# Feed-forward down projections: nine of eleven row pairs by seven block products, six pairs' sums made beside gate and up and kept in DRAM

## The chip, the cores and the metric

The kernel runs on one core of a Trainium2 chip. The metric is the device time of one execution in microseconds (us). It computes in float32: every weight block is split into a high and a low part, so that one float32 product takes three matmuls on TensorE (PE): high by high, high by low, low by high.

## The reference, cut to what matters

Two layers (`L = 2`) of an encoder on x of 256 tokens by 1024. Each layer has a feed-forward half step, a mixing block (two attentions and gates, not touched here), and a second feed-forward half step. So a feed-forward block runs four times.

```python
x = x + 0.5 * swiglu(rms_norm(x, ffn1_norm[l]), ffn1_w_gate[l], ffn1_w_up[l], ffn1_w_down[l])
...
x = x + 0.5 * swiglu(rms_norm(x, ffn2_norm[l]), ffn2_w_gate[l], ffn2_w_up[l], ffn2_w_down[l])

def swiglu(x, w_gate, w_up, w_down):
    return (jax.nn.silu(x @ w_gate) * (x @ w_up)) @ w_down
```

`w_gate` and `w_up` are 1024 x 2816, `w_down` is 2816 x 1024.

## The kernel before, in words

A feed-forward block (`ffn`, L305) has two stages.

**Gate and up.** The 2816 hidden columns are cut into eleven chunks of 256 (`NFC`). For each chunk c the loop at L429 loads four pieces of weights, 512 KB each (`columns`, L143; `load`, L137), and multiplies both halves of the tokens with them (`project`, L270): 2 x 24 matmuls of 128x512. ScalarE (ACT) and VectorE (DVE) make the hidden values `hh` from that (L443, L445). Some time later, by a lag counted in blocks of three matmuls (`H_LAG`, and `LAST_LAG` for the last chunk), `turn` (L310) transposes them on PE and splits them.

**Down.** `down` (L372) goes over the same eleven chunks, each now a pair of 128-row blocks of `w_down`. A pair is a product of 2x2 blocks of the tokens' hidden values by 2x2 blocks of weights. The table `PLAN` says how each pair is done:

- S: eight block products, two rows of weights, 24 matmuls (`out_rows`, L286).
- F and G: seven block products (Strassen's scheme in Winograd's form), 21 matmuls (`sevens`, L359, and the loop at L384). They need sums and differences of blocks on both sides. On the side of the hidden values `turn` makes them: seven slots instead of four, by four additions of 128x128 and a larger split. On the side of the weights four differences of 128x512 make two tiles u and v (`differences`, L341).
- G makes u and v in the down stage from the two rows it loads. F has had them made beside gate and up (`prepare`, L352): at the chunks that are keys of `PREP`, for the pair that is the value, two more rows are loaded, u and v are made and split, and both parts stay in SBUF (`stored`). In the down stage an F pair loads only half of its first row and its second row.

The plan before is `SFGFGFGSGSS`: seven pairs by seven products, of which three are F.

**What sets the order.** PE's order is the program's. On the other engines a scheduler orders the instructions; within an engine they run in that order, and each waits for its inputs and for its buffer. All weight loads, also those of `prepare`, are issued from SyncE's queue (SP) into four slots of 512 KB, `raw` (`RAW = 4`). ScalarE makes the high part (L182) and VectorE the low part (L183) into six slots each, `wh` and `wl` (`RING = 6`). A `raw` slot is free when VectorE has read it the last time; a `wh`/`wl` slot when PE has used it. The first block of each seven (`corner`, L363) has a place of its own in the tiles of the normalized tokens. Sums of the hidden values, u, v and the final combination (`combine`, L403) share two buffers, `sums`.

GpSimd (POOL) makes the identity at the start, the reciprocal roots of the norms (`rsqrt`, L172), small work of the attention, and issues six small DMAs.

Of the kernel before, what the change touches and what calls it, by code (L numbers as in the profile page):

```python
# [41 lines left out]
RAW = 4  # L42
LAG = 3
H_LAG, NORM_LAG, QK_LAG, P_LAG, V_LAG, M_LAG = 7.9, 4.0, 16, 10, 7.5, 5.5
LAST_LAG = 6.1
ORDER = ("Q0 Q1 K0 K1 q1 q0 a4 k0 a5 k1 a3 v0 a1 a5 v1 a3 g0 a1 a5 g1 a4 g2 a0 g3 a0 a4 g4 a1 a5 g5 a4 "
         "g6 a0 g7")
FMAX = 3.0e38
IN_W = 4352
HEAD = 128  # L50
PLAN = "SFGFGFGSGSS"
PREP = {2: 1, 5: 3, 8: 5}
NS = sum(kind != "S" for kind in PLAN)


@with_exitstack
def hybrid_encoder(ctx, tc, x, w_gu1, w_d1, w_in, b_gate, qk_gain, rpb, sink, t5,
# [11 lines left out]

    def pad(pool, name, nbytes):  # L70
        nc.vector.memset(pool.tile([P, nbytes // 4], F32, name=name, tag=name, bufs=1), 0.0)

    pad(small, "pad_s", 256)

    wide = act.tile([P, HEAD + D], F32, name="x0", tag="x0")
    gain = wide[:, :3 * L * KD].rearrange("p (n k) -> p n k", n=3 * L)
# [93 lines left out]
        nc.tensor.matmul(ps, xl, wh, start=False, stop=last)  # L170
# [134 lines left out]
    def ffn(l, n, w_gu, w_d, after):  # L305
        with tc.tile_pool(name="ffn", bufs=1) as fp:
# [1 line left out]
            SLOT = ((1, 2), (0, 3))  # L308

            def turn(c, hh):  # L310
                tp = ps_tp.tile([P, 4, P], F32, name="tp", tag="tp")
                for t in range(T):
                    for i in range(2):
                        nc.tensor.transpose(tp[:, SLOT[t][i], :], hh[t][:, i * P:(i + 1) * P], ident)  # L314
                m = 4 if PLAN[c] == "S" else 7
                hi = fp.tile([P, m, P], F32R, name=f"hi{m}", tag=f"hi{m}", bufs=NS if m == 7 else NFC - NS)
                lo = fp.tile([P, m, P], F32R, name=f"lo{m}", tag=f"lo{m}", bufs=NS if m == 7 else NFC - NS)
                if m == 7:
                    a = fp.tile([P, 8, P], F32, name="a", tag="sums", bufs=2)
                    nc.scalar.activation(a[:, :4, :], tp, AF.Copy)  # L320
                    for to, x, y, op in ((4, 0, 3, ALU.add), (6, 1, 0, ALU.subtract), (5, 4, 1, ALU.subtract),
                                         (7, 2, 5, ALU.subtract)):
                        nc.vector.tensor_tensor(a[:, to, :], a[:, x, :], a[:, y, :], op)
                    split_to(hi, lo, a[:, 1:, :])
                else:
                    with tc.high_priority(150 if c == NFC - 1 else 0):
                        split_to(hi, lo, tp)
                hs[c] = (hi, lo)

            def get(t, k):  # L330
# [9 lines left out]

            def differences(r0, r1, into):  # L341
                sub = lambda to, x, y: nc.vector.tensor_tensor(to, x, y, ALU.subtract)  # L342
                u = fp.tile([P, 2, 512], F32, name="u", tag="sums", bufs=2)
# [3 lines left out]
                v = fp.tile([P, 2, 512], F32, name="v", tag="sums", bufs=2)  # L347
# [24 lines left out]
            def down():  # L372
# [4 lines left out]
                while c < NFC:  # L377
                    if PLAN[c] == "S":
                        end = NFC if "S" * (NFC - c) == PLAN[c:] else c + 1
                        out_rows(get, acc, 2 * c, 2 * end, end == NFC, w_d, l, 0.5, after, *rest)  # L380
                        c = end
                        continue
                    final = c == max(PLAN.rindex("F"), PLAN.rindex("G"))
                    for name, slot, (wh, wl) in sevens(c):  # L384
                        if name in banks:
                            t, d = banks[name]
                            first = acc[t][d] is None
                            if first:
                                acc[t][d] = out_bank(t, d)
                            bank = acc[t][d]  # L390
                        else:
                            first = name not in extra
                            if first:
                                pool, tag = (ps_g, "g") if name in "16" else (ps_tp, "tp")
                                extra[name] = pool.tile([P, 512], F32, name=tag, tag=tag)
                            bank = extra[name]
                        three(bank, *[h[:, slot, :] for h in hs[c]], wh, wl, first, final and name in extra)
                        tick(1)
                    if final:
                        rest.append(combine(extra))  # L400
                    c += 1

            def combine(acc):  # L403
                p1, p16 = [fp.tile([P, 2, 512], F32, name=n, tag="sums", bufs=2) for n in ("p1", "p16")]
# [24 lines left out]
            for c in range(NFC):  # L429
# [5 lines left out]
                else:  # L435
                    pieces = columns(w_gu, l, c * 512, 512)
                if c in PREP:
                    prepare(PREP[c])
                pair = []
                for t in range(T):  # L440
                    ps = both[t] if first else project(t, pieces, 512)
# [2 lines left out]
                    hh = fp.tile([P, FC], F32, name="hh", tag="hh", bufs=2)  # L444
                    nc.vector.scalar_tensor_tensor(hh, ps[:, FC:], rstd[t], sg, op0=ALU.mult, op1=ALU.mult)  # L445
# [378 lines left out]
```

## Time and profile before

| what | us |
|---|---|
| median of 3 runs (lowest, highest) | 1088.5 (1087.56, 1088.72) |
| the profiled execution | 1088.83 |
| its span, first to last instruction | 1087.1 |
| second feed-forward block: ten chunks of gate and up | 113.7 (from 372.2 to 485.9) |
| the same block: down | 53.6 (from 490.3 to 543.9) |

One core is profiled; the granted clock of TensorE is 1.000 over the whole span. Times in rows are microseconds from the span's start unless the row says ns. In the table of windows a row holds, for a stretch of time, its length and then the busy time and the number of instructions of PE, PE's weight loads (PEld), DVE, ACT and POOL, then the granted clock, the mean busy share of the 16 DMA engines, and the rate that they moved. In the rows of groups, what stands after the bar is the busy time in us and the mean ns of one, and after the second bar the engine's idle time before them with what ended it. In the rows of DMA issues stand the count, the size of one and the median us from issue to landing. Matmuls overlap, so their rate is read from start to start and not from their duration.

### The profile page before, as it was taken

To read this page: it belongs to the slowest core of one execution; us is meant where nothing else is said; L and a number is where in the kernel's file an instruction comes from. 1 tells how busy PE (TensorE), PEld (TensorE's weight loads), DVE (VectorE), ACT (ScalarE), POOL (GpSimd) and SP (SyncE) were. 2 spreads that over 40 slices of the span, in tenths; PEclk is the share of its full clock that TensorE was granted. 3 is DMA by queue.
4 is the path that set the end of the run, shared out by engine and by line. 5 is a ranking of instruction groups with operands and counts; after the bars stand their busy time and mean duration, and the time that the engine had idled before them with its cause. 6 is when DMAs were issued, how large, how long until landed. Compare 5 with 4: busy or idle time off the path is not lost.

```text
span 1087.1 us, 14699 instructions
## 1 busy us (share of the span) xinstructions
PE 1075.3 (99%) x5137; PEld 891.5 (82%) x5137; DVE 854.8 (79%) x1298; ACT 659.3 (61%) x1002; POOL 116.4 (11%) x118
## 2 busy tenths in 40 slices
PE   9999999999999999999999999999999999999998
PEld 6888888888888888888878888888888888888887
DVE  6888788889886778778877777888888767878785
ACT  6665654788764556565465656457877645656542
POOL 1400000243510000000000000003534000000000
PEclk9999999999999999999999999999999999999999
DMA  7876665755654676666657766547566555776652
GB/s 243 265 218 211 196 200 174 238 186 151 193 179 136 199 227 207 210 203 203 194 174 222 223 211 204 177 155 241 178 188 187 171 169 162 222 241 196 211 167 94
DMA packets 98828, 212.63 MB, mean 196 GB/s; under 512 B 7569, under 2 KB 13745, under 8 KB 98753
## 3 DMA queue, kind: packets, MB, share of 16 engines
q1 hardware_dynamic: 98560, 211.60, 62.3%
q8 instruction: 40, 0.66, 0.2%
q14 instruction: 36, 0.29, 0.1%
q0 software_dynamic: 192, 0.08, 0.1%
HBM read 210.59 MB, written 1.06 MB: 195 GB/s over the span
## 4 chain that ended last, share of the span: by engine, by line
PE 85%; DVE 8%; ACT 3%; issue 3%; DMA 1%; POOL 0%; ACTq 0%; DVEq 0%
PE g L168 19%; PE g L170 19%; PE g L169 18%; PE acc L168 6%; PE acc L170 6%; PE acc L169 6%; DVE wl L183 3%; PE tp L314 2%; ACT wh L182 1%; PE tp L169 1%; PE tp L170 1%; PE tp L168 1%; DMA raw<-in_w_d 1%; PE pt L568 1%; PE sc L547 1%
## 5 line engine op out<-in xcount | busy, mean ns | idle before, releaser
L183 DVE TENSOR_TENSOR wl<-raw,wh 128x1024 fp32r<-128x1024 f32 (+1 forms) x340 | 408.0, 1215 | 75.6 <-ACT wh L182 74.5
L182 ACT ACTIVATE wh<-raw 128x1024 fp32r<-128x1024 f32 (+1 forms) x340 | 348.8, 1044 | 117.4 <-PE g L170 39.3
L168 PE MATMUL g<-wh,xh 128*128 128x512 f32 (+1 forms) x976 | 386.1, 396 | 0.0
L170 PE MATMUL g<-wh,xl 128*128 128x512 f32 (+1 forms) x976 | 378.2, 387 | 0.7 <-DVE xl L183 0.7
L169 PE MATMUL g<-wl,xh 128*128 128x512 f32 (+1 forms) x976 | 377.9, 387 | 0.8 <-DVE wl L183 0.8
L170 PEld LDWEIGHTS g<-wh,xl 128*128 128x128 f32 x976 | 183.4, 188 | 40.8 <-DVE xl L183 2.1
L169 PEld LDWEIGHTS g<-wl,xh 128*128 128x128 f32 x976 | 183.9, 188 | 33.8 <-DVE wl L183 1.6
L168 PEld LDWEIGHTS g<-wh,xh 128*128 128x128 f32 x976 | 183.6, 188 | 32.5 <-DVE hh L445 0.2
L443 ACT ACTIVATE sg<-g,rs_y 128x256 f32<-128x256 f32 x88 | 41.2, 468 | 102.9 <-PE g L170 102.6
L342 DVE TENSOR_TENSOR u<-raw 128x512 f32<-128x512 f32 x56 | 38.5, 690 | 64.5 <-DMA raw<-in_w_d 64.1
L168 PE MATMUL acc<-wh,hi 128*128 128x512 f32 x200 | 78.9, 394 | 0.0
L170 PE MATMUL acc<-wh,lo 128*128 128x512 f32 x200 | 77.9, 390 | 0.0
L169 PE MATMUL acc<-wl,hi 128*128 128x512 f32 x200 | 77.9, 390 | 0.0
L174 POOL TENSOR_TENSOR rs_y<-ms,mhalf 128x1 f32<-128x1 f32 x12 | 6.6, 554 | 657.3 <-DVE ms L220 648.9
L445 DVE SCALAR_TENSOR_TENSOR hh<-g,rs_y,sg 128x256 f32<-128x256 f32 x88 | 42.2, 479 | 28.8 <-ACT sg L443 28.8
L182 ACT ACTIVATE corner<-raw 128x512 fp32r<-128x512 f32 x28 | 17.6, 629 | 62.3 <-DMA raw<-in_w_d 47.0
L560 POOL TENSOR_TENSOR S<-S,sm 128x512 f32<-128x512 f32 x32 | 37.1, 1159 | 71.5 <-DVE sm L559 45.4
L170 PEld LDWEIGHTS acc<-wh,lo 128*128 128x128 f32 x200 | 37.6, 188 | 8.0
L168 PEld LDWEIGHTS acc<-wh,hi 128*128 128x128 f32 x200 | 37.6, 188 | 7.5
L169 PEld LDWEIGHTS acc<-wl,hi 128*128 128x128 f32 x200 | 37.6, 188 | 7.5
L553 ACT ACTIVATE S<-S,mx 128x256 f32<-128x256 f32 x64 | 31.8, 498 | 7.5 <-DVE mx L550 7.4
L174 POOL TENSOR_TENSOR rs_y<-hv,mhalf 128x8 f32<-128x8 f32 (+1 forms) x16 | 27.0, 1693 | 31.4 <-DVE hv L476 28.4
(190 smaller groups left out, 1462.9 us busy)
## 6 DMA issues: line engine op xcount, KB each, us to landing
raw<-in_w_gu SPq DMA_DIRECT2D x176, 512.0 KB, 4.4
raw<-in_w_d SPq DMA_DIRECT2D x100, 512.0 KB, 4.4
raw<-in_w_in SPq DMA_DIRECT2D x64, 512.0 KB, 4.5
raw<-in_w_out SPq DMA_DIRECT2D x16, 512.0 KB, 3.5
bb<-in_b_gate SPq DMA_DIRECT2D x16, 256.0 KB, 3.4
raw<-in_w_bsw SPq DMA_DIRECT2D x8, 512.0 KB, 3.7
raw<-in_w_bna SPq DMA_DIRECT2D x8, 512.0 KB, 3.6
raw<-in_w_d SPq DMA_DIRECT2D x12, 256.0 KB, 2.6
```

Of the source, the lines that this page charges most:

```text
L168: nc.tensor.matmul(ps, xh, wh, start=first, stop=False)
L169: nc.tensor.matmul(ps, xh, wl, start=False, stop=False)
L170: nc.tensor.matmul(ps, xl, wh, start=False, stop=last)
L174: rstd_done[0] = nc.gpsimd.tensor_tensor(y, v, mhalf[:, :n], ALU.pow)
L182: linked("act", lambda: nc.scalar.activation(hi, src, AF.Copy))
L183: linked("dve", lambda: nc.vector.tensor_tensor(lo, src, hi.bitcast(F32), ALU.subtract))
L314: nc.tensor.transpose(tp[:, SLOT[t][i], :], hh[t][:, i * P:(i + 1) * P], ident)
L342: sub = lambda to, x, y: nc.vector.tensor_tensor(to, x, y, ALU.subtract)
L443: nc.scalar.activation(sg, ps[:, :FC], AF.Silu, scale=rstd[t])
L445: nc.vector.scalar_tensor_tensor(hh, ps[:, FC:], rstd[t], sg, op0=ALU.mult, op1=ALU.mult)
L553: nc.scalar.activation(S_[:, t, :], S_[:, t, :], AF.Exp, bias=mx[:, t:t + 1], scale=-1.0, accum_out=sm[:, t:t + 1])
L560: nc.gpsimd.tensor_tensor(S_, S_, sm.unsqueeze(2).to_broadcast([P, T, S]), ALU.mult)
```

## The change

The plan becomes `FHHGHHHHFSS`: nine pairs by seven products, in three kinds. There are two F pairs (0 and 8), one G pair (3) and six of a new kind, H (1, 2, 4, 5, 6, 7); the last two stay S.

- For H, u and v are made beside gate and up as for F, but not split: they are stored to DRAM as they are. In the down stage they are loaded again into `raw` slots and split there. An H pair therefore loads, in the down stage, half a row, a row, u and v: four `raw` slots, where F takes two (half a row and a row), G and S two rows.
- Pairs are prepared at eight chunks (2 to 9) instead of three. Their two rows no longer go through `raw` and SyncE's queue, but through two buffers of their own, `beside`, loaded by DMAs from GpSimd's queue, which also issues the stores of u and v. Per block that is 16 loads and 12 stores of 512 KB on GpSimd's queue.
- The rows of a pair are asked for at the start of a chunk's code and the differences made at its end, behind both `hh`.
- `sums` has three buffers instead of two. To make room, a pad and part of a small tile go, and the scratch for descriptors of GpSimd's DMAs is halved.
- As the plan now begins with a seven-product pair, its accumulators take the banks that the last turn used. The last `turn` transposes into an accumulator bank that is taken ahead (`spare`), with the same lag as the others.

```diff
-PLAN = "SFGFGFGSGSS"
-PREP = {2: 1, 5: 3, 8: 5}
+PLAN = "FHHGHHHHFSS"
+PREP = {2: 0, 3: 1, 4: 2, 5: 8, 6: 4, 7: 5, 8: 6, 9: 7}
+SUMS = 3
...
-    pad(small, "pad_s", 256)
...
-        y = small.tile([P, 24], F32, name="rs_y", tag="rs_y")[:, :n]
+        y = small.tile([P, 8], F32, name="rs_y", tag="rs_y")[:, :n]
...
+    spare = []
+
     def out_bank(t, d):
+        if t and d and spare:
+            return spare.pop()
         tag, n = ACC[t][d]
...
             def turn(c, hh):
-                tp = ps_tp.tile([P, 4, P], F32, name="tp", tag="tp")
+                if c == NFC - 1:
+                    spare.append(out_bank(1, 1))
+                    tp = spare[0].rearrange("p (i n) -> p i n", i=4)
+                else:
+                    tp = ps_tp.tile([P, 4, P], F32, name="tp", tag="tp")
...
-            def prepare(c):
+            def beside(k):
+                r = fp.tile([P, 2, 512], F32, name="beside", tag="beside", bufs=2)
+                nc.gpsimd.dma_start(r, w_d[l, k * P:(k + 1) * P, :].rearrange("p (h n) -> p h n", h=2))
+                return r
+
+            def prepare(c, rows2):
                 def into(name, r):
+                    if PLAN[c] == "H":
+                        kept = dram.tile([P, 2, 512], F32, name=f"{name}{l}{n}{c}")
+                        nc.gpsimd.dma_start(kept, r)
+                        return kept
                     hl = [fp.tile([P, 2, 512], F32R, name=f"{name}{p}{c}", tag=f"{name}{p}{c}") for p in "hl"]
                     split_to(*hl, r)
                     return hl
-                stored[c] = differences(block_row(2 * c), block_row(2 * c + 1), into)
+                stored[c] = differences(*rows2, into)
 
             def sevens(c):
+                def fetched(kept):
+                    r = ring.tile([P, 2, 512], F32, name="raw", tag="raw", bufs=RAW)
+                    nc.sync.dma_start(r, kept)
+                    return parts(r)
...
                 us, vs = stored.get(c) or differences(r0, r1, lambda name, r: parts(r))
+                if PLAN[c] == "H":
+                    us, vs = fetched(us), fetched(vs)
...
                 if c in PREP:
-                    prepare(PREP[c])
+                    rows2 = [beside(2 * PREP[c] + i) for i in range(2)]
...
-                defer(LAST_LAG if c == NFC - 1 else H_LAG, ("h", c), lambda c=c, pair=pair: turn(c, pair))
+                defer(H_LAG, ("h", c), lambda c=c, pair=pair: turn(c, pair))
+                if c in PREP:
+                    prepare(PREP[c], rows2)
...
-    nc = _bacc.Bacc("TRN2", target_bir_lowering=False, num_devices=1, dynamic_dma_scratch_size=2048)
+    nc = _bacc.Bacc("TRN2", target_bir_lowering=False, num_devices=1, dynamic_dma_scratch_size=1024)
```

How the change moves instructions is shown at two places. The first is SyncE's queue in the down stage of the first block, before, from the third pair on (a G pair's two rows, an F pair's half row and row, a G pair's two rows, and so on; L338 is `block_row`, and `raw` is numbered by the program):

```order
L338 DMA raw_1389<-in_w_d1 128x1024
L338 DMA raw_1391<-in_w_d1 128x1024
L338 DMA raw_1435<-in_w_d1 128x512
L338 DMA raw_1437<-in_w_d1 128x1024
L338 DMA raw_1467<-in_w_d1 128x1024
L338 DMA raw_1469<-in_w_d1 128x1024
L338 DMA raw_1513<-in_w_d1 128x512
L338 DMA raw_1515<-in_w_d1 128x1024
```

The same queue now, from the G pair (3) through the first two of the four H pairs behind it (4 and 5); u004 and v004 are the stored differences of pair 4, and L376 is where they are fetched:

```order
L343 DMA raw_1516<-in_w_d1 128x1024
L343 DMA raw_1518<-in_w_d1 128x1024
L343 DMA raw_1562<-in_w_d1 128x512
L343 DMA raw_1564<-in_w_d1 128x1024
L376 DMA raw_1573<-u004_949 128x1024
L376 DMA raw_1579<-v004_954 128x1024
L343 DMA raw_1606<-in_w_d1 128x512
L343 DMA raw_1608<-in_w_d1 128x1024
L376 DMA raw_1617<-u005_1060 128x1024
L376 DMA raw_1623<-v005_1065 128x1024
```

Eight rows of the queue covered four pairs before; ten rows cover three pairs now.

The second place is GpSimd's queue at the program's start. Before, the identity is made at once, and the first DMAs are the small constants (`rs_y` are the reciprocal roots of the first norm):

```order
masks.py:197 MEMSET ident_85 128x128
masks.py:199 ISA
masks.py:199 AFFINE_SELECT ident_85<-ident_85 128x128
L174 TENSOR_TENSOR rs_y_216<-ms_213,mhalf_92 128x1
L174 TENSOR_TENSOR rs_y_229<-ms_226,mhalf_92 128x1
L103 DMA qkg_96<-in_qk_gain 128x8
```

Now the two rows of the pair that is prepared at chunk 2 stand in between:

```order
masks.py:197 MEMSET ident_83 128x128
L359 DMA beside_388<-in_w_d1 128x1024
L359 DMA beside_390<-in_w_d1 128x1024
masks.py:199 ISA
masks.py:199 AFFINE_SELECT ident_83<-ident_83 128x128
L172 TENSOR_TENSOR rs_y_214<-ms_211,mhalf_90 128x1
L172 TENSOR_TENSOR rs_y_227<-ms_224,mhalf_90 128x1
L101 DMA qkg_94<-in_qk_gain 128x8
```

The two loads moved ahead of the identity, to the very start of the execution.

More of the change, by code (lines that the diff above doesn't have):

```diff
@@ L318, in turn @@
                 if m == 7:
-                    a = fp.tile([P, 8, P], F32, name="a", tag="sums", bufs=2)
+                    a = fp.tile([P, 8, P], F32, name="a", tag="sums", bufs=SUMS)
                     nc.scalar.activation(a[:, :4, :], tp, AF.Copy)
@@ L325, in turn @@
                 else:
-                    with tc.high_priority(150 if c == NFC - 1 else 0):
-                        split_to(hi, lo, tp)
+                    split_to(hi, lo, tp)
                 hs[c] = (hi, lo)
@@ L342, in differences @@
                 sub = lambda to, x, y: nc.vector.tensor_tensor(to, x, y, ALU.subtract)
-                u = fp.tile([P, 2, 512], F32, name="u", tag="sums", bufs=2)
+                u = fp.tile([P, 2, 512], F32, name="u", tag="sums", bufs=SUMS)
                 sub(u[:, 0, :], r1[:, 1, :], r0[:, 1, :])
@@ L346, in differences @@
                 us = into("u", u)
-                v = fp.tile([P, 2, 512], F32, name="v", tag="sums", bufs=2)
+                v = fp.tile([P, 2, 512], F32, name="v", tag="sums", bufs=SUMS)
                 sub(v[:, 0, :], r1[:, 1, :], u[:, 1, :])
@@ L382, in down @@
                         continue
-                    final = c == max(PLAN.rindex("F"), PLAN.rindex("G"))
+                    final = c == len(PLAN.rstrip("S")) - 1
                     for name, slot, (wh, wl) in sevens(c):
@@ L403, in combine @@
             def combine(acc):
-                p1, p16 = [fp.tile([P, 2, 512], F32, name=n, tag="sums", bufs=2) for n in ("p1", "p16")]
+                p1, p16 = [fp.tile([P, 2, 512], F32, name=n, tag="sums", bufs=SUMS) for n in ("p1", "p16")]
                 ends = act.tile([P, 512], F32, name="ends", tag="xg", bufs=2)
```

1 line of the change is left out of this document (removed).

## The prediction

> **What bounds the kernel now.** I read the page's busy shares first, then TensorE's waits, then the two stages of one feed-forward block in the table of windows.
>
> ```profile
> PE 1075.3 (99%) x5137; PEld 891.5 (82%) x5137; DVE 854.8 (79%) x1298; ACT 659.3 (61%) x1002; POOL 116.4 (11%) x118
> PE pt L568 <- DVE sm L559: 2.0, 2, 1.0
> ...
> PE tp L314 <- DVE hh L445: 0.4, 1, 0.4
> 372.20:485.90 113.70, 113.58 (x520) 93.53 (x519) 86.11 (x121) 68.32 (x88) 0.56 (x1) 1.00 0.67 214
> 490.30:543.90 53.60, 53.60 (x244) 44.38 (x243) 44.33 (x54) 25.40 (x31) 0.00 (x0) 1.00 0.62 197
> ```
>
> The first row is the page's; the next two are the first and last of seven rows of TensorE's waits (total, times, longest), which run from 2.0 down to 0.4 us, so under 14 us in 1087. The last two are windows: ten chunks of gate and up of the second block, and its down projection. TensorE is busy throughout at full clock; VectorE is at 76% and 83%, the DMA engines at 0.67 and 0.62. The kernel is TensorE's stream of matmuls. So the change can gain what it takes out of that stream and nothing else, and can lose wherever data come later than the stream wants them.
>
> The pace of the stream, from two rows of the timeline, one pair (21 matmuls) apart:
>
> ```profile
> 505.38 0.39 PE L168 MATMUL g<-corner,hi 128*128 128x512 f32 x1
> 510.14 0.39 PE L168 MATMUL g<-corner,hi 128*128 128x512 f32 x1
> ```
>
> 4.76 us for 21 matmuls is 0.227 us each; the 0.39 us shown overlap. A chunk of gate and up takes 113.7 / 10 = 11.37 us.
>
> **The sum is made against** the profiled execution: 1088.83 us, of which the span is 1087.1. It is 0.3 us above the median of the runs, and I take that off at the end.
>
> **Taken out.** A pair by eight products is 24 matmuls, by seven 21. Two more pairs per block go by seven; four blocks; 2 x 3 x 4 = 24 matmuls fewer, which is also what the order of TensorE shows. 24 x 0.227 = **-5.4 us**, all on the path. Transposes stay equal in number.
>
> **VectorE**, per block, by these groups (mean ns in the second place behind the bar):
>
> ```profile
> L183 DVE TENSOR_TENSOR wl<-raw,wh 128x1024 fp32r<-128x1024 f32 x332 | 402.8, 1228 | 75.3 <-ACT wh L182 74.3
> L182 ACT ACTIVATE wh<-raw 128x1024 fp32r<-128x1024 f32 x332 | 344.2, 1054 | 116.7 <-PE g L170 38.6 <-DMA raw<-in_w_gu 36.0 <-PE acc L170 14.2
> L445 DVE SCALAR_TENSOR_TENSOR hh<-g,rs_y,sg 128x256 f32<-128x256 f32 x88 | 42.2, 479 | 28.8 <-ACT sg L443 28.8
> L342 DVE TENSOR_TENSOR u<-raw 128x512 f32<-128x512 f32 x56 | 38.5, 690 | 64.5 <-DMA raw<-in_w_d 64.1
> L183 DVE TENSOR_TENSOR lo<-a,hi 128x896 fp32r<-128x896 f32 x28 | 30.4, 1084 | 0.0
> L323 DVE TENSOR_TENSOR a<-a 128x128 f32<-128x128 f32 x112 | 27.5, 287 | 1.9
> 519.80 2.35 DVE L183 TENSOR_TENSOR wl<-raw,wh 128x1024 fp32r<-128x1024 f32 x2
> ```
>
> The last row, two splits back to back in 2.35 us, shows that consecutive instructions overlap by 0.1 us (2 x 1.22 - 2.35). A chunk that prepares an H pair holds four splits, two hh, the four sums and the split of a seven-slot turn, and four differences: 4 x 1.228 + 2 x 0.479 + 4 x 0.287 + 1.084 + 4 x 0.690 = 10.9 us, less 15 overlaps of 0.09, 9.5 us of TensorE's 11.37. The two chunks that prepare F pairs add two splits, 11.8 us; before there were three such. In the down projection an H pair needs a corner split (half of 1.228) and three full ones, 4.3 us of 4.76, where a G pair needed four differences more. VectorE stays off the path: **0**. ScalarE, with 1.05 us per split, has less in each chunk than VectorE.
>
> **The down projection's loads** are what I worry about. They all pass through four `raw` slots; a slot is free again when VectorE has split what it held.
>
> ```profile
> raw<-in_w_d SPq DMA_DIRECT2D x100, 512.0 KB, 4.4
> raw<-in_w_d SPq DMA_DIRECT2D x19, 512.0 KB, 4.1
> DMA to landing us min/median/max: 3.6/3.6/4.9
> raw<-in_w_d SPq DMA_DIRECT2D x6, 512.0 KB, 4.2
> raw<-in_w_d SPq DMA_DIRECT2D x2, 256.0 KB, 2.6
> 480.27 0.33 SPq L338 DMA_DIRECT2D raw<-in_w_d  x1
> 481.79 0.33 SPq L338 DMA_DIRECT2D raw<-in_w_d  x1
> 488.20 0.33 SPq L338 DMA_DIRECT2D raw<-in_w_d  x1
> 491.67 0.33 SPq L338 DMA_DIRECT2D raw<-in_w_d  x1
> ```
>
> The first three rows are the time from issue to landing of a full row: in the whole kernel, in the down stage (468 to 530), and of five loads at 515 to 530. The two after them are the loads of the down weights that were out between 468 and 490.3, eight in all. The four issues are of one G pair's two rows and of the loads that took their slots: held 7.9 and 9.9 us.
>
> An F pair asks for a half row and a row, S and G pairs for two rows, an H pair for a half row and three rows: four slots per 4.76 us. So each slot must turn round in 4.76 us. It needs landing + 1.05 (ScalarE) + 1.22 (VectorE): 5.9 us at the lone 3.6, 6.4 at 4.1, 6.7 at 4.4, 7.2 at 4.9. Every H pair thus loses 1.1, 1.6, 1.9 or 2.4 us of its lead, and the plan has two H pairs, a G pair and then four H pairs.
>
> The lead in front of those four: eight loads are out before the stage begins at 490.3, and the same eight places cover the first F and H pairs and part of the third. The G pair's second row then goes out some 3.6 us into the stage, behind the splits of the third pair, and holds its slot 8 to 10 us; so the last load of the fifth pair (the first of the four) goes out at about 12 us and is split at 12 + 6.7 = 18.7. TensorE wants it at 4 x 4.76 + 4 products of 0.68 = 21.8. The lead is 3.1 us, then 1.2, -0.7 and -2.6: TensorE waits 2.6 us in a block. At a landing time of 4.1 it waits 1.4, at 3.6 nothing, at 4.9 4.6. The load behind, an F pair, asks for less and adds nothing. With four loads to a pair the busier median is nearer, so I take 4.4: 4 x 2.6 = **+10.4 us** (ends 0 and 18.4).
>
> **The start.** The first two `beside` loads stand on GpSimd's queue ahead of the identity, and nothing holds them back.
>
> ```profile
> 2.00:12.00 10.00, 9.84 (x40) 6.75 (x40) 5.04 (x6) 4.52 (x11) 0.00 (x0) 1.00 0.99 357
> 5.78 0.63 ACT L182 ACTIVATE xh<-xg 128x512 fp32r<-128x512 f32 x1 [3.55 <-DVE xg L206]
> 6.31 1.04 ACT L182 ACTIVATE wh<-raw 128x1024 fp32r<-128x1024 f32 x1
> 22.07 0.56 POOL L104 DMA_DIRECT2D mask<-in_c_mask  x1
> ```
>
> From 2 to 12 us the DMA engines are full (0.99) at 357 GB/s, and 1.05 MB more are 2.9 us of that. If every first load slides by it, that is the price; if ScalarE, back to back at 5.78 and 6.31, hides it, nothing. I take the middle, **+1.5 us**. The issue itself (0.56 us on GpSimd) delays the identity by 1.1 us, before x has landed: 0.
>
> **What is hidden.** A store of sums on GpSimd's queue waits for VectorE, and behind it stand the next pair's row and the other store; the row is fetched a chunk (11.37 us) ahead, so its landing of some 4.4 us has 7 to spare. Behind the first `beside` loads of a later block stands the reciprocal root for its first chunk, 2 x 0.56 us later at most; its first reader comes after a pass of 24 matmuls, 5.4 us: 0. The fetches on SyncE's queue wait for stores made more than a chunk before: 0. The last turn goes to a spare accumulator bank and 1.8 ticks later, for a pair some 45 us ahead: 0. The first product needs a g bank that was read a pass earlier: 0. Smaller pads and half the descriptor scratch are not to be seen in this trace; a stall there would sit on GpSimd's queue with the same 7 us of cover.
>
> **Sum:** 1088.8 - 5.4 + 10.4 + 1.5 = 1095.3, less 0.3: **1095 us**. Its own range is 1089 (waits of 1.1 us a block) to 1104 (4.6 us and the full start).
>
> **Rivals.**
>
> *The lead is never used up* (the other side). If loads in the run of H pairs land in 3.6 us, as the lone ones do, the slot turns in 5.9 us, the lead falls from 3.9 by 1.1 a pair and stays above zero. It decides at about 3.8 us. For it: half of the loads at 515 to 530 landed in 3.6. Against it: the stage's median is 4.1 with half as many loads. Then 1088.8 - 5.4 + 1.5 - 0.3 = 1084.6, with 1083 to 1086 for the start's ends.
>
> *The DMA engines become the bound beside gate and up.* A chunk that prepares an H pair moves 2.10 MB of its own, 1.05 of rows and 1.05 of stores: 4.19 MB in 11.37 us, 369 GB/s. The fullest row above gave 357: 11.75 us, 0.38 late in each of six chunks, 9 us in four blocks. The gate and up row extrapolates lower, 214 / 0.67 = 319 GB/s: 13.1 us, 1.8 late, 43 us. Rows prefetched a chunk ahead take up much of a backlog, so I price it near the lower end, 15 us on top of the forecast: 1110. The Trainium skill, "DMA: Bandwidth & Descriptors", section "Issuing engines are not separate DMA queues", speaks against the change in this sense: loads issued from another engine run on the same sixteen DMA engines and save only issue time. No run here shows two full queues. The same page, section "Where 436 GB/s comes from", puts HBM's share of a core at about 358 GB/s, and the trace agrees with 357 at 0.99; by that figure alone the estimate for this rival would be 8 us and not 15.
>
> *Gain and loss cancel.* Waits of about 1 us a block give back the 5.4: 1088.5, no change.
>
> **How the numbers follow.** The forecast has 0.45, the unused lead 0.30, the DMA bound 0.15, cancelling 0.10. A measurement of this kernel tells about 0.2% (2.2 us) from no change. Faster is the second case, 0.30; the same is cancelling and 0.03 of the forecast's low edge, 0.13; slower is the rest, 0.57. The range 1083.5 to 1106 holds nearly all of the first, second and fourth case and the low end of the third. As both signs count, the likeliest case's own range, 1089 to 1104, stands beside it.
>
> **What would show it.** Right: the page counts 5113 matmuls; TensorE's waits name wl, split from raw, at the "2" to "4" products of the seventh and eighth pair; a down stage is longer than 53.6 us less 1.4; the pitch of the first three pairs is 4.76 us and of the eighth over 6. Wrong: TensorE's waits stay under 14 us in all (the lead lasts); or a chunk of gate and up takes over 11.7 us with DMA at 0.95 or more (the DMA bound); or VectorE waits for `beside` for more than a few us per block.

## The result, and the profile after

| | median, us | runs | ratio to before, 95% interval |
|---|---|---|---|
| before | 1088.6 | 1087.6 to 1089.9 | |
| after | 1134.7 | 1127.3 to 1138.5 | 1.041 [1.037, 1.046] |

After is 46 us slower: the sign that was forecast, but seven times the 6.5 us of the forecast, and far outside the range. Its runs spread over 11 us where those of before spread over 2. The profiled execution is the quickest of them, 1127.3 us with a span of 1125.5, so the trace can show 38.4 us of the 46.

First the page's busy shares and traffic of after.

```profile
span 1125.5 us, 15135 instructions
...
PE 1083.9 (96%) x5113; PEld 889.4 (79%) x5113; DVE 898.6 (80%) x1377; ACT 682.7 (61%) x1026; POOL 172.2 (15%) x230
...
HBM read 251.48 MB, written 26.23 MB: 247 GB/s over the span
```

There are 24 matmuls fewer, as counted, but TensorE is busy for 96% of the span and no longer 99%. Where it went idle shows in a table of windows: the four down projections (from the first block product to the last matmul into an accumulator), then the second layer's first gate and up. Before:

```profile
135.50:192.30 56.80, 56.80 (x258) 46.94 (x258) 47.02 (x59) 27.45 (x35) 0.56 (x1) 1.00 0.57 179
489.90:546.70 56.80, 56.80 (x258) 46.94 (x257) 46.71 (x59) 27.69 (x35) 0.55 (x1) 1.00 0.59 188
673.10:729.80 56.70, 56.70 (x258) 46.87 (x257) 46.86 (x59) 27.79 (x35) 0.55 (x1) 1.00 0.57 179
1027.70:1083.40 55.70, 55.70 (x248) 45.80 (x246) 42.28 (x51) 22.19 (x26) 0.00 (x0) 1.00 0.46 150
546.90:673.10 126.20, 125.54 (x575) 103.40 (x574) 97.35 (x136) 76.24 (x100) 0.55 (x1) 1.00 0.67 209
```

The same five stages after:

```profile
137.90:203.00 65.10, 57.94 (x252) 45.10 (x251) 48.49 (x55) 35.48 (x42) 0.00 (x0) 1.00 0.74 244
500.20:567.40 67.20, 60.50 (x252) 47.61 (x252) 49.19 (x56) 35.45 (x42) 0.00 (x0) 0.95 0.75 248
693.20:760.50 67.30, 60.79 (x252) 47.30 (x251) 49.17 (x56) 35.47 (x42) 0.00 (x0) 0.95 0.72 241
1059.20:1121.80 62.60, 56.74 (x242) 44.12 (x240) 43.84 (x49) 29.94 (x34) 0.00 (x0) 1.00 0.66 225
567.60:693.20 125.60, 125.55 (x575) 103.42 (x574) 106.20 (x159) 73.97 (x98) 16.09 (x30) 1.00 0.85 294
```

Gate and up, with all its new work beside it, took 125.6 us where it took 126.2: TensorE is full there, VectorE has 106 of 125.6 and the DMA engines 0.85. The down projections took 262.2 us where they took 226.0. That is 36.2 of the 38.4 us; nearly all of the rest lies ahead of the first of them (it begins at 137.9 and not at 135.5). In two of the four the granted clock is 0.95.

TensorE's waits of after (total us, times, longest), the rows that before lacks:

```profile
PE g L166 <- DVE hh L466: 11.1, 5, 3.0
PE acc L167 <- DVE wl L181: 5.4, 9, 0.8
PE g L167 <- DVE wl L181: 5.2, 8, 0.8
PE g L166 <- ACT wh L180: 4.8, 5, 2.0
PE tp L197 <- DVE x L301: 2.4, 2, 1.2
...
PE tp L197 <- DMA x<-in_x: 1.4, 1, 1.4
```

These are 30.3 us in 30 waits. The waits for `wl` and `wh` (15.4) are the late splits that the prediction spoke of: 10.0 us in the pairs, on the seventh and eighth, and 5.4 us on the eight-product rows at the stage's end, into `acc`. The largest row is another one: a matmul into a `g` bank waits for `hh`, the product of the last gate and up pass. One of the five lies at the kernel's start (2.9 us), the other four at the beginning of a down projection. There the timeline of the second block reads, on four engines (start, duration, engine, operation, and in brackets the idle time before it and what ended it):

```profile
498.14 0.32 SPq L376 DMA_DIRECT2D raw<-v  x1
...
503.32 1.06 ACT L180 ACTIVATE wh<-raw 128x1024 fp32r<-128x1024 f32 x1 [3.63 <-DMA raw<-v]
504.28 0.46 ACT L464 ACTIVATE sg<-g,rs_y 128x256 f32<-128x256 f32 x1
...
504.41 1.23 DVE L181 TENSOR_TENSOR wl<-raw,wh 128x1024 fp32r<-128x1024 f32 x1 [2.96 <-ACT wh L180]
505.55 0.48 DVE L466 SCALAR_TENSOR_TENSOR hh<-g,rs_y,sg 128x256 f32<-128x256 f32 x1
...
506.08 0.50 PE L166 MATMUL g<-vh,hi 128*128 128x512 f32 x1 [2.95 <-DVE hh L466]
...
508.18 0.63 PE L167 MATMUL tp<-ul,hi 128*128 128x512 f32 x1
508.61 0.63 PE L168 MATMUL tp<-uh,lo 128*128 128x512 f32 x1
```

The last pass of gate and up ended at 500.25, where the first product starts. Its `sg` could have run at once, but on ScalarE it stands behind the split of the second pair's `v`, and that split waits for a load issued at 498.14 that came in at 503.3. `hh` on VectorE stands behind the other half of the same split. Product "6", the fifth of the first pair, needs the bank that `hh` frees.

Before, the same two instructions, behind a pass that ended at 489.93:

```profile
490.44 0.46 ACT L443 ACTIVATE sg<-g,rs_y 128x256 f32<-128x256 f32 x1
493.30 0.48 DVE L445 SCALAR_TENSOR_TENSOR hh<-g,rs_y,sg 128x256 f32<-128x256 f32 x1
```

There `sg` ran almost at once, and `hh` stood behind VectorE's splits too, but no product needed a `g` bank before 495.83, since the stage began with a pair by eight products.

The last two rows of after's timeline show something more: behind the stall the matmuls follow each other by 0.43 us and not by 0.227. A window over the stretch shows why.

```profile
507.00:510.50 3.50, 3.50 (x11) 2.63 (x10) 2.19 (x3) 1.50 (x2) 0.00 (x0) 0.55 0.86 289
```

The granted clock is 0.55 over these 3.5 us. The trace has four such stretches, from 507.4, 544.9, 698.5 and 749.7, and windows of 3.3 us laid into them show 0.50 each. Over the whole trace 32 matmuls stand 0.43 us apart where before had 5: 27 x 0.2 = 5.4 us. With 30.3 us of waits, 30 x 0.16 for the overlap that each wait loses (0.39 shown, 0.227 pitch) and 5.4 of gain this makes 35 of the 38.4 us; a gap of some 0.1 us on the matmul behind a wait accounts for most of the rest.

### The profile page after: what moved, and what is told of

It is laid out like the page before. It is cut to its first block, busy times and chain, and to the rows that moved or that the text cites. A ratio compares the mean times of both kernels' runs of the same rounds, so it can differ in the third digit from the quotient of the medians.

```text
span 1125.5 us, 15135 instructions
## 1 busy us (share of the span) xinstructions
PE 1083.9 (96%) x5113; PEld 889.4 (79%) x5113; DVE 898.6 (80%) x1377; ACT 682.7 (61%) x1026; POOL 172.2 (15%) x230
## 4 chain that ended last, share of the span: by engine, by line
PE 55%; DMA 17%; DVE 15%; ACT 7%; issue 6%; POOL 0%; SPq 0%; ACTq 0%; DVEq 0%; POOLq 0%
PE g L168 14%; PE g L166 14%; PE g L167 14%; DVE wl L181 8%; DMA raw<-v 8%; ACT wh L180 5%; DMA raw<-in_w_d 4%; PE acc L167 2%; PE acc L168 2%; PE acc L166 2%; DMA beside<-in_w_d 2%; DMA raw<-in_w_gu 2%; PE tp L320 1%; PE pt L591 1%; PE tp L197 1%
## 5 line engine op out<-in xcount | busy, mean ns | idle before, releaser
L181 DVE TENSOR_TENSOR wl<-raw,wh 128x1024 fp32r<-128x1024 f32 (+1 forms) x380 | 457.6, 1216 | 119.7 <-ACT wh L180 118.3
L180 ACT ACTIVATE wh<-raw 128x1024 fp32r<-128x1024 f32 (+1 forms) x380 | 393.3, 1047 | 219.9 <-PE g L168 55.7
L359 POOL DMA_DIRECT2D beside<-in_w_d x64 | 34.5, 539 | 263.3 <-DVE u L347 95.1
L347 DVE TENSOR_TENSOR u<-beside 128x512 f32<-128x512 f32 x64 | 43.3, 686 | 30.8 <-DMA beside<-in_w_d 22.7
L166 PE MATMUL acc<-wh,hi 128*128 128x512 f32 x164 | 65.7, 401 | 0.0
L168 PE MATMUL acc<-wh,lo 128*128 128x512 f32 x164 | 64.9, 396 | 0.0
L366 POOL DMA_DIRECT2D u<-u x24 | 12.9, 538 | 216.2 <-DVE u L347 183.1
L180 ACT ACTIVATE hi<-a 128x896 fp32r<-128x896 f32 x36 | 33.9, 942 | 12.9 <-DVE a L329 12.9
L181 DVE TENSOR_TENSOR lo<-a,hi 128x896 fp32r<-128x896 f32 x36 | 39.3, 1092 | 0.0
L329 DVE TENSOR_TENSOR a<-a 128x128 f32<-128x128 f32 x144 | 36.2, 285 | 1.8
```

The costliest lines, as they stand in the source:

```text
L166: nc.tensor.matmul(ps, xh, wh, start=first, stop=False)
L180: linked("act", lambda: nc.scalar.activation(hi, src, AF.Copy))
L181: linked("dve", lambda: nc.vector.tensor_tensor(lo, src, hi.bitcast(F32), ALU.subtract))
L359: nc.gpsimd.dma_start(r, w_d[l, k * P:(k + 1) * P, :].rearrange("p (h n) -> p h n", h=2))
L366: nc.gpsimd.dma_start(kept, r)
```

## The experiments

Theories. **A**: four `raw` slots are too few for four loads a pair. **B**: the added traffic makes loads land later. **C**: the plan begins with a seven-product pair, which needs both gate banks at once. **D**: on ScalarE and VectorE, instructions that free a bank stand behind splits that wait for a load.

| run | what it is | median, us | ratio to before, 95% interval |
|---|---|---|---|
| e1_apart | fetched sums in slots of their own | 1107.9 | 1.017 [1.012, 1.021] |
| e2_sfirst | plan begins with an eight-product pair | 1144.0 | 1.051 [1.048, 1.053] |
| e3_bare | nothing beside gate and up for H pairs | 1122.6 | 1.033 [1.031, 1.035] |
| e4_nostore | no stores, plain rows fetched | 1119.4 | 1.029 [1.027, 1.030] |
| e5_order | second pair's splits behind the last `hh` | 1139.8 | 1.048 [1.046, 1.050] |
| e6_late | first two beside loads later | 1132.0 | 1.040 [1.039, 1.042] |
| e7_apart_order_late | e1, e5 and e6 together | 1098.1 | 1.009 [1.008, 1.011] |
| e8_floor | e7 without stores | 1094.5 | 1.006 [1.005, 1.008] |
| e9_gorder | e7, fifth pair's splits behind the fourth's | 1101.8 | 1.013 [1.011, 1.016] |
| e10_allorder | e7, every pair's splits behind the last pair's | 1094.9 | 1.006 [1.005, 1.008] |
| e11_nog | e7, an eight-product pair for the G pair | 1088.5 | 1.000 [0.999, 1.001] |
| e12_prep10 | e10, the G pair made an H pair | 1128.0 | 1.035 [1.034, 1.037] |
| e13_nog_allorder | e10 and e11 | 1089.7 | 1.001 [1.000, 1.002] |
| e14_nog_nostore | e11 without stores | 1086.1 | 0.998 [0.997, 0.999] |

### Slots: e1_apart

```diff
-                def fetched(kept):
-                    r = ring.tile([P, 2, 512], F32, name="raw", tag="raw", bufs=RAW)
+                def fetched(kept, tag, bufs):
+                    r = fp.tile([P, 2, 512], F32, name="back", tag=tag, bufs=bufs)
...
-                    us, vs = fetched(us), fetched(vs)
+                    us, vs = fetched(us, "beside", 2), fetched(vs, "sums", SUMS)
```

> The kept sums come back into slots of their own (u into the two idle beside slots, v into the three sums slots), so the four raw slots serve two loads of an H pair and not four; bytes, queues and order of loads are as after. Theory A, too few slots: TensorE's waits for wl and wh in the down projections, 20 us in the trace of after, fall under 4 us, the wait for the last gate (9 us) and the half-speed matmuls behind stalls (6 us) mostly go as well, because loads are out sooner: 1084 to 1094 us. Theory B, landing times lengthened by the added traffic: 1115 to 1135, since the traffic is the same. Theory C, the plan that begins with a seven-product pair: the wait for the last gate's bank stays at 9 us and more, 1100 to 1110.

Measured 1107.9 (1101.5 to 1112.3): 27 us less than after with the same bytes. Its waits of TensorE:

```profile
PE g L166 <- DVE hh L466: 15.7, 5, 4.2
PE tp L320 <- DVE hh L466: 2.8, 3, 1.6
```

No row for `wl` or `wh` is left, 15.4 us in after: theory A holds for these. But the wait for `hh` grew from 11.1 to 15.7 us, and the time is not in A's range but in C's. Slots are one cause of two. They don't help by sooner landing: the fetched sums took a median of 6.3 (u) and 5.5 us (v) to land, where after's took 4.2 and 4.4.

### Order of the plan: e2_sfirst

```diff
-PLAN = "FHHGHHHHFSS"
-PREP = {2: 0, 3: 1, 4: 2, 5: 8, 6: 4, 7: 5, 8: 6, 9: 7}
+PLAN = "SFHHGHHHHFS"
+PREP = {2: 1, 3: 2, 4: 3, 5: 9, 6: 5, 7: 6, 8: 7, 9: 8}
+LAST_LAG = 6.1
```

> The plan begins with an eight-product pair as before (SFHHGHHHHFS), and the last turn is again as before; same number of products, loads and bytes. Theory C, the early use of both gate banks is the cause: the wait for the last gate goes with its half-speed matmuls, about 9 plus 4 us, 1118 to 1123 or lower, the other waits as in after. Theory A, too few slots: the shortage only moves, waits for wl grow by about what the other loses: 1122 to 1140. Theory B: as after, 1130 to 1140.

The last turn's lag, bank and priority are as in before, too. Measured 1144.0, 9 us more than after and above all three ranges. The first rows of TensorE's waits:

```profile
PE tp L198 <- DVE x L302: 12.6, 3, 4.3
PE tp L317 <- DVE hh L464: 6.8, 4, 2.2
```

No block product waits for the last `hh` any more, but `hh` is as late as it was: now the last turn's transposes wait for it (second row), in all four stages. So C falls as it was put. The plan decides which matmul waits for the last `hh`, not that it is late; in before the turns waited 0.4 us in all. The first row is a new cost: one eight-product pair is left at the end instead of two, and the norm's transposes wait up to 4.3 us for the update of x that sums up the seven products. That the shorter end is the reason was not tested apart.

### Traffic: e3_bare, e4_nostore

For e3 the six H pairs get no rows, differences or stores beside gate and up; e4 makes the differences and stores nothing:

```diff
-                        kept = dram.tile([P, 2, 512], F32, name=f"{name}{l}{n}{c}")
-                        nc.gpsimd.dma_start(kept, r)
-                        return kept
+                        k = 2 * c + (name == "v")
+                        return w_d[l, k * P:(k + 1) * P, :].rearrange("p (h n) -> p h n", h=2)
```

> For the six H pairs nothing is made beside gate and up: no rows, no differences, no stores; the down projection fetches plain rows of the down weights into the same raw slots at the same places (so its result is not the layer's). Theory A: the down stages lose as much as in after; only what gate and up lost, some 6 us, comes back: 1122 to 1133. Theory B: landing times near those of before, 1084 to 1100. Theory C: the gate bank's wait stays, 9 us and its half speed, 1095 to 1110.

> Rows are loaded and differences made beside gate and up as in after, but no H sums are stored, and plain rows of the down weights are fetched instead (so the result is not the layer's): 25 MB of writes less, the same loads. Theory A: 1125 to 1136. Theory B, if the stores are the part of the traffic that hurts: 1090 to 1115. Theory C: as after.

Measured 1122.6 and 1119.4, both outside B's range and in or below A's: with 25 MB of reads and 25 MB of writes gone (e3), or the writes alone (e4), the kernel is still 34 or 31 us slower than before. So traffic is not most of what makes it slow. It is not free either: without the stores 15 us come back (8 between the two traces). Loads on GpSimd's queue land sooner, by the table of DMA issues (last number, median us from issue to landing), after first:

```profile
beside<-in_w_d POOLq DMA_DIRECT2D x64, 512.0 KB, 6.5
```

and the run without stores:

```profile
beside<-in_w_d POOLq DMA_DIRECT2D x64, 512.0 KB, 4.7
```

On SyncE's queue these two runs can't be set side by side, because without stores the fetches are counted with the rows of the down weights. Two later runs that differ in the stores alone, e7 and then e8, have the same 56 loads:

```profile
raw<-in_w_d SPq DMA_DIRECT2D x56, 512.0 KB, 5.2
```

```profile
raw<-in_w_d SPq DMA_DIRECT2D x56, 512.0 KB, 4.3
```

That e3, which does less, is 3 us over e4 wasn't settled; the waits for `hh` are longer in e3 (12.1 us, and 7.7 in e4).

### Queue order and start: e5_order, e6_late

e5 queues the second pair's splits behind the last `sg` and `hh` (issue order only, no wait):

```diff
+                    with ExitStack() as behind:
+                        if c == 1:
+                            behind.enter_context(tc.issue_after(gate_out[0].ins))
+                            behind.enter_context(tc.issue_after(gate_out[1].ins))
+                        blocks = sevens(c)
```

> Only the order on ScalarE and VectorE is changed: the second pair's splits are queued behind the last chunk's gate (sg) and product (hh), which after puts behind splits that still wait for their load; slots, loads and bytes as after. Theory D, the queue order at the stage's start: the wait for the last hh, 8.9 us in the trace of after, falls under 2 us and some 3 us of half-speed matmuls go with it: 1120 to 1126. Theory A alone, the shortage only moves: splits of the second pair come later, waits for wl grow by as much, 1130 to 1138.

Measured 1139.8: the answer of theory A, just above its range. Its waits of TensorE:

```profile
PE acc L167 <- DVE wl L181: 11.8, 14, 1.4
PE g L167 <- DVE wl L181: 9.8, 19, 0.8
PE tp L167 <- DVE wl L181: 6.6, 11, 0.8
PE g L166 <- DVE hh L472: 2.9, 1, 2.9
```

The `hh` wait is gone at all four stages (the one left is the kernel's start), and the waits for `wl` and `wh` grew from 15.4 us to 28.2 for `wl` alone. So theory D is right about this wait, and it is worth nothing alone. A split that comes later frees its `raw` slot later; with too few slots the order only chooses where TensorE waits.

e6 puts the kernel's first two beside loads behind the first reciprocal root:

```diff
+                        if n == 0 and c == 2:
+                            behind.enter_context(tc.issue_after(rstd_done[0].ins))
```

> The first two beside loads of the kernel are queued behind the first reciprocal root on GpSimd, some 18 us later, and the first gate stands ahead of two splits on ScalarE again, as in before; nothing else. If the start costs what the trace shows (1.6 us for the second piece of x, 3.1 us for the first hh), the first hh is back at 26.3 us with neither wait and the median is 4 to 6 us under after's: 1128 to 1131. Rival: the loads only move, the rows come late for the third chunk's differences and TensorE waits there instead: 1133 to 1136.

Measured 1132.0, between the two forecasts and 2.7 us less than after; after's own spread doesn't let the runs tell that from nothing. In the trace the 2.9 us wait for the first `hh` is gone and the first chunk's second `hh` ends at 25.1 us and not at 26.5. What had delayed it was again ScalarE's order. After's timeline at the start:

```profile
20.17 1.99 ACT L180 ACTIVATE wh<-raw 128x1024 fp32r<-128x1024 f32 x2
22.06 0.45 ACT L464 ACTIVATE sg<-g,rs_y 128x256 f32<-128x256 f32 x1
...
24.05 0.50 PE L166 MATMUL g<-wh,xh 128*128 128x512 f32 x1 [2.92 <-DVE hh L466]
```

and that of before:

```profile
19.23 0.47 ACT L443 ACTIVATE sg<-g,rs_y 128x256 f32<-128x256 f32 x1 [0.19 <-PE g L235]
```

Two loads more on GpSimd's queue made the scheduler put the first `sg` behind two splits, on an engine that the loads never touch; with the loads moved it stands ahead of them again.

### All three: e7_apart_order_late, e8_floor

> Slots of their own for the fetched sums, the queue order at the stage's start, and the late first loads, all three. Theories A and D together, nothing else being at work: all added waits go, 1088.6 less 5.4 plus at most 6 for what is left: 1083 to 1090. Theory B, traffic: TensorE still waits for loads, 1093 to 1105.

> As the run with all three edits, and the sums aren't stored; plain rows of the down weights are fetched in their place (so the result is not the layer's). If the stores' traffic costs something of its own, this is over 4 us faster than the run with all three edits; if it only hurt through the slots and the queue order, within 3 us of it: 1082 to 1088.

Measured 1098.1 and 1094.5. Together they take 37 of after's 46 us away: slots alone took 27, the later loads 3, and order, which alone made it 5 us worse, the rest. The stores cost 3.6 us here and no longer 15, just under the 4 us that the expectation asked for. But neither run reached the forecast of theories A and D; e7 is in theory B's range, and in both TensorE still waits at one product in each down projection. e7's first waits, and the timeline of VectorE and ScalarE in the second block:

```profile
PE g L166 <- ACT wh L180: 4.3, 4, 1.5
PE g L167 <- DVE wl L181: 3.8, 6, 0.8
```

```profile
509.49 0.69 DVE L348 TENSOR_TENSOR v<-raw,v 128x512 f32<-128x512 f32 x1
...
510.27 0.63 ACT L180 ACTIVATE corner<-raw 128x512 fp32r<-128x512 f32 x1 [4.19 <-DMA raw<-in_w_d]
510.81 1.04 ACT L180 ACTIVATE wh<-v 128x1024 fp32r<-128x1024 f32 x1
```

It is the G pair, whose sums are made in the down projection. On ScalarE the split of its `v` stands behind a corner that waits for a load; by the order of the loads it is the sixth pair's, two pairs further on. But the corner is only part of it: VectorE itself finished `v` only at 510.18, so without the corner its split could start 0.6 us sooner at most, of the 1.5 us that TensorE waits there.

### The G pair: e9_gorder, e10_allorder, e11_nog

e9 and e10 queue splits behind the last split of the pair ahead (`if c == PLAN.index("G") + 1:` and `if c > 1:`); e11 changes the plan alone:

```diff
-PLAN = "FHHGHHHHFSS"
+PLAN = "FHHSHHHHFSS"
```

> The run with all three edits, and the splits of the fifth pair are queued behind the G pair's last split on ScalarE and VectorE. There TensorE still waited 2.5 us a block for the G pair's v, whose split stood behind a corner that waited for its load. Theory D, queue order: those waits (9 us) and some 3 us of half-speed matmuls go: 1085 to 1090. Theory A, slots: the G pair still holds its raw slots for 8 to 10 us, the next loads are as late as before and TensorE waits at the fifth or sixth pair instead: 1094 to 1099.

> As the run before, with every pair's splits from the third on queued behind the last split of the pair ahead of it. If other inversions cost as well, 1 to 4 us under that run; if they cost nothing, within 2 us; if the strict order makes ready splits wait for late loads, over it by 2 or more.

> The run with all three edits, with an eight-product pair in the G pair's place (FHHSHHHHFSS): 12 matmuls more, 2.7 us, and no differences in the down projection. If the G pair's place is all that is left to lose, its 9 us and 3 us of half speed go: 1088 to 1092. If slots are still short without it, TensorE waits at the pairs behind: 1096 to 1101.

e9 measured 1101.8, no better than e7 and above both of its ranges. It says little about order, because it moves the fifth pair's splits, and the corner in the way is the sixth's. In e9's second block that still stands ahead of the split of `v`, which runs at 516.65:

```profile
516.11 0.63 ACT L182 ACTIVATE corner<-raw 128x512 fp32r<-128x512 f32 x1 [4.14 <-DMA raw<-in_w_d]
```

e10, which orders every pair, takes it out of the way. It measured 1094.9, 3 us under e7 and 7 under e9, more than its forecast. Its waits for `wl` and `wh`, 5.8 us in all, are still the G pair's but for 0.4 us, and now `v` itself is what is late (second block):

```profile
507.89 0.69 DVE L350 TENSOR_TENSOR v<-raw,v 128x512 f32<-128x512 f32 x1
...
508.67 1.06 ACT L182 ACTIVATE wh<-v 128x1024 fp32r<-128x1024 f32 x1 [2.99 <-PE acc L168]
```

Its split starts 0.1 us after VectorE has made it, and TensorE still waits 0.5 us for that and 0.8 us for the low part. e11 measured 1088.5, with 12 matmuls more than e10, within its forecast. Its first waits:

```profile
PE pt L600 <- DVE sm L591: 2.1, 2, 1.0
PE tp L197 <- DVE x L301: 1.8, 1, 1.8
```

The first stands in before as well, the second is one late update of x; for `wl` and `wh` one wait of 0.4 us is left, at the kernel's start, as in before. So the G pair in the middle of H pairs was what remained. How much of that is its differences on VectorE and how much its hold on the `raw` slots was not separated.

### What is left: e12_prep10, e13_nog_allorder, e14_nog_nostore

e12 makes the G pair an H pair, its sums made beside the last chunk (`PLAN = "FHHHHHHHFSS"`, `10: 3` added to `PREP`).

> The ordered run (slots of their own, queue order from pair to pair, late first loads) with the G pair made into an H pair whose sums are made beside the last chunk (FHHHHHHHFSS): nine pairs by seven products and no differences in the down projection; 4.2 MB of rows and 4.2 MB of stores more. If the G pair's differences and its hold on the raw slots were what remained (7 us of waits in four blocks): 1083 to 1088, under before. If the last chunk's added rows and stores delay the stage's start instead: 1092 to 1102.

> The ordered run with an eight-product pair in the G pair's place (FHHSHHHHFSS). Against the same plan without the order from pair to pair (1088.5): if inversions there still cost, 1 to 3 us less, 1085 to 1088; if the strict order costs, 1089 to 1092.

> The plan without a G pair (FHHSHHHHFSS, slots, order at the stage's start, late first loads), and the sums aren't stored; plain rows of the down weights are fetched in their place (so the result is not the layer's). If the stores' traffic still has a price of its own once nothing waits for a slot, 2 to 4 us less than with them: 1084 to 1087. If it only hurt through late loads that something stood behind, the same as with them within 1.5 us.

e12 measured 1128.0, far above both of its ranges. Its first waits:

```profile
PE tp L166 <- ACT wh L182: 16.2, 4, 4.4
PE g L166 <- DVE hh L480: 7.6, 5, 1.8
```

The last chunk's rows hold the two beside slots into the down projection; the second pair's `u` needs one of them, is issued at 508.9, 7 us into the stage, and lands at 515.1. That is theory A at another place, and behind these waits of 3.5 to 4.4 us the granted clock is down again (0.50 over windows of 6.5 us in three of the four stages).

e13 measured 1089.7: order from pair to pair gives nothing more without the G pair. e14 measured 1086.1, within its forecast; 12 matmuls fewer than before are 2.7 us, and 1088.4 - 2.7 = 1085.7. So without stores, and with slots and order in place, the count of matmuls gives the time within 0.4 us, and the stores' own price is about 2.4 us, e11 less e14. No kernel that computes the layer beat before by what can be measured: e11 is at 1.000.

## Why the prediction was wrong, point by point

- **TensorE's stream, -5.4**: right. 5113 matmuls, and e14, with 12 fewer than before and no wait in its down projections, is 2.3 us under before, where 12 x 0.227 is 2.7.
- **VectorE, 0**: right; gate and up took 125.6 us with 106 us of VectorE in it.
- **The down projection's slots, +10.4**: for the pairs the mechanism, the place and the size were right. They lost 10.0 us by the waits view (5.2 for `wl`, 4.8 for `wh`) at the seventh and eighth pair, on product "6", for which the lead had been worked out. Of the signs named for it, the eighth pair's pitch was 7.1 to 8.8 us in three stages and 5.8 in the other, but the first pair's was 6.1 to 9.4 and not 4.76. "The load behind, an F pair, asks for less and adds nothing" failed: the eight-product rows behind it wait another 5.4 us, and the norm another 2.4 for the update of x. Taking the shortage away was worth 27 us, e1 against after.
- **A wait at its own length**: the sum priced each wait so and had no term for more. By the working above, the 30 waits lost some 8 us besides, in overlap and slow restart, and 5.4 us went with half-speed stretches.
- **"The first product needs a g bank that was read a pass earlier: 0"**: the step that failed. It priced product "1". Product "6" takes the other bank, 2.7 us after the last pass ends, and that bank is free only when `sg` and `hh` have run; these stand behind splits of the second pair, on ScalarE and VectorE. I followed the new waits on GpSimd's and SyncE's queues and not the new splits on ScalarE's. Four such waits cost 8 us, and a half-speed stretch came with two of them. Their cause is not the slots, since in e1 they grow, and not the plan alone, since in e2 others wait for the same `hh`; e5 takes them away by order alone.
- **The start, +1.5**: the size was near (2.4 us before the first down projection), most of it by ScalarE's order and not by the DMA engines.
- **What is hidden, 0**: not contradicted for the stores on GpSimd's queue, the rows, the fetches' wait for stores and the smaller pads: nothing in TensorE's waits names them. VectorE did wait for `beside`, 22.7 us in 18 waits or 5.7 a block, which the prediction had listed as a sign of being wrong; no chunk lost time by it.
- **The DMA engines as the bound beside gate and up**: fell; 0.85 and 294 GB/s there, and no chunk lost time. What that rival had right is that side traffic makes the others' loads land later: the stores cost 15 us in after, 2.4 to 3.6 once slots and order give slack. On the Trainium skill's rule from "DMA: Bandwidth & Descriptors", section "Issuing engines are not separate DMA queues", that DMAs issued by different engines run on the same 16 DMA engines, the traces agree: with stores on GpSimd's queue the same 56 loads on SyncE's queue took 5.2 us to land (e7), without them 4.3 (e8).
- **The lead is never used up** (the other side): the case that e14 shows, at 1086.1, but it needs more slots, an order by hand, no G pair and no stores.

Of the 32 us by which the trace passes the sum, the bank's wait is 8, the rows behind the pairs and the norm are 8, what waits cost besides is 13, and the start's waits (2.9 and 1.4 us against 1.5) are 3.

Two causes, then, each of which covers the other. With few slots, order only moves the wait (e5: +5 us); with slots, the wrong order still costs the bank's wait (e1: 15.7 us); both, with the later first loads, give 37 us back (e7), the G pair 10 more (e11). Left open: why the runs of after, e1 and e11 spread over 9 to 11 us and those of before and e14 over 3 and 1. For after the clock has a part in it: from its quickest run to its slowest the granted clock falls from 0.994 to 0.986. At half clock for 3.4 us and some 1.4 us lost a stretch (5.4 / 4), that is an estimated five stretches more and 7 of the 11 us. In e11 the clock is 0.999 to 1.000 in every run, so its spread is something else.

## What to carry to other kernels

When a plan moves the stage that comes first, ask which bank or buffer its first few operations take, which instruction frees that, and what stands ahead of that instruction on its own engine: a freeing instruction behind a split that waits for a load waits for the load. When loads per unit of work go up, count the slots against landing plus both halves of the split, for the rows behind the run as well. And test slots and order together: each alone can look useless or harmful.

## What the runs showed of the hardware

A stall of TensorE can cost more than itself. In after's trace the granted clock fell to 0.50 for 3.4 us four times, some 1.4 us lost each time. Two came with single waits of 2.95 and 3.00 us (507.4 and 698.5), two behind three shorter waits close together: 1.6 us of waits in all between 542.2 and 545.0, and 1.8 us between 745.3 and 749.0. The length of a wait alone doesn't decide it. The one of 2.92 us at the start of after left the clock up, those of 2.93 to 2.95 us at the same place in e1, e4 and e5 didn't; in e3 the clock fell at 504.86 behind a single one of 1.85 us (ended at 504.06), in e11 it stayed up behind one of 1.75 us (ended at 542.02). The Trainium skill, "TensorE: Matmul & The Clock Gate", section "HAM oscillation — how this bites in real kernels", puts the abstract rule at no idle gaps of over some 3.4 us; here shorter ones were enough at times, and the measurement decides.

The DMA engines went past the 357 GB/s that the prediction took for their most. e11, at the beginning of its third down projection (window, DMA share, GB/s at the end of the row):

```profile
679.50:706.70 27.20, 27.20 (x123) 22.52 (x122) 22.35 (x23) 19.10 (x23) 0.00 (x0) 1.00 0.98 375
```

375 GB/s over 27 us, and TensorE didn't wait once in it. So neither 357 nor the 358 GB/s cited beside it in the prediction is a bound here; the measurement decides.
